# Buffers in two stacks that hand tiles on between the phases of a GLA and conv-FFN block

## The chip, the cores and the metric

The kernel runs on one core of a Trainium2 chip. The time is that of one execution on the device, in microseconds (us), median of several. The engines that matter: PE (TensorE, matmuls and transposes), DVE (VectorE), ACT (ScalarE), POOL (GpSimd), and SP (SyncE), whose queue issues nearly all DMAs in order.

## The reference

One block on a sequence of 2048 tokens with 1024 channels, in float32: a gated linear attention (GLA, 4 heads), then a feed-forward network with a causal convolution of 3 taps, each with a residual, and a last RMS norm.

```python
h = rmsnorm(x, mix_norm_w[i])
y = gla_mixer(h, gla_w_in[j], gla_w_gate2[j], gla_b_gate[j], gla_norm_w[j], gla_w_out[j])
x = x + y.astype(x.dtype)
h = rmsnorm(x, ffn_norm_w[i])
x = x + conv_ffn(h, ffn_w_up[i], ffn_conv_w[i], ffn_conv_b[i], ffn_w_down[i]).astype(x.dtype)
return rmsnorm(x, final_norm_w)

def conv_ffn(h, w_up, conv_w, conv_b, w_down):
    u = causal_dwconv(h @ w_up, conv_w, conv_b)
    g, val = jnp.split(u, 2, axis=-1)
    return (jax.nn.silu(g) * val) @ w_down
```

`w_up` is 1024 x 5632 and `w_down` 2816 x 1024.

## The kernel before

Every float32 matrix product is made of three matmuls: `split` (L206, L207) cuts an operand into a high part (a cast on ACT) and a low part (a subtraction on DVE), and high x low, low x high and high x high are added in PSUM. There are three phases.

**Attention** runs over four blocks of 512 tokens (b = 0 to 3) and, in each, over four heads. The class `Weights` streams all weights of the phase through two rings of buffers of the pool `wp`: "raw" (what DMAs bring, RB = 3) and "w" (the split halves, WB = 18). `hp` has two tiles of 16 KB a partition (the halves of the transposed activations, `hT`), `op` those of the heads' results (`oT`), rows and a ring of 2 KB tiles "s2k" (SB = 15), `sp` and `gc` smaller tiles and constants. `comp_y(b, dh, ...)` multiplies with the output weights in two halves of the channels (`py`, L333 to L335), adds the residual (`x`, L590) and, after the second half, norms the rows for the FFN (`h`, L595). Work that needs such a result much later is put off: `later_do` pushes it on a heap `delayed`, and `adv(us)`, called from attention's matmul helper `mm3` with the estimated time of the matmuls, takes out what is due. One such piece is `blocks`: it transposes the rows on PE (`pt_d`, L604), and for each pair of row tiles makes the seven operands of the next phase (POOL differences `ht`, L621; splits `h_p`, L207) and writes both halves of each to DRAM (`hd`, L617): 14 writes.

**U** multiplies with `w_up` by seven block products p1 to p7 instead of eight. It runs for two halves of the sequence, s = 0 and 1, and in each over 11 groups g; a group has 14 jobs, the products in the order `OPS` = p1, p5, p6, p2, p7, p4, p3 for two column tiles f. A job has 12 matmuls (L714 to L716, in `mm3p`) of one weight operand (`uw_p`) and one activation operand (`h_p`, read from `hd`, L824 and L834). The weights of a group come in four loads (`ur`, L743, ring of 6), POOL makes the sums of blocks (`us`, L748, ring of 5), `split` the halves (ring of 14), five jobs ahead (ULEAD). `ua`, `uc`, `ub` are the products in PSUM. The results are put together in `u`, convolved (`t`, L789 to L793), gated (L798), and the seven operands of the next phase are made by POOL (`as`, L812 to L816) and written to DRAM (`ad`, L802 to L818).

**D** multiplies with `w_down`, again by seven products, in 14 units (product, s) of 11 steps q with 12 matmuls each (`pd`). A step loads its activations (`da`, L905, ring of 7) ten steps ahead and splits them four steps ahead (DLEAD, DLOAD), and for s = 0 the weights too: `ch` is a running combination of blocks in 11 tiles, `dr` a raw block (tag "wr", ring of 6), `dw` their halves (26 buffers).

The Python program gives instructions in this order, and a scheduler then orders each engine's stream by estimated times; the order is fixed when the kernel is built, and each engine, SP's queue too, goes through its own in order. A pool that is opened over the space of a closed one waits for the tiles that lay there. Between the phases, space is handed over pool by pool:

```python
    while delayed:
        heapq.heappop(delayed)[-1]()
    gctx.close()
    ...
    for s in range(NS):
        phase_u(s)
    uctx.close()
```

So `gctx` with all attention pools is closed after the last delayed work, then U's pools `uw`, `uh`, `us` are opened over them; `uctx` is closed after U, then D's `dx`, `dw`, `ds` are opened.

## Time and profile before

| | before |
|---|---|
| time, median of 3 executions (lowest to highest) | 2300.17 us (2300.15 to 2302.63) |
| the profiled execution | 2300.66 us, span 2299.0 us, mean granted PE clock 0.977 |
| first matmul of U, first of D | 985.29 us, 1869.2 us after the start of the span |
| DMA | 322.84 MB, mean 140 GB/s |

Times in the prediction are those of the span of the profiled execution. A row of the timeline has the start, the duration, the engine, the line, the operation, out<-in, how many were put together, and in brackets how long the engine sat idle before it and what released it. In a row of the waits stand the engine and what it waited for, then the sum in us, the number of times and the longest. In the windows, the busy times are those of PE, PEld (weight loads), DVE, ACT and POOL with the number of instructions; then come the clock granted to PE as a share of full speed, the DMA share and GB/s. The rows of DMA issues have KB each and the median us from issue to landing. Line numbers are those of the kernel before; the line numbers of the changed kernel are larger (L714 to L716 become L733 to L735, L604 becomes L607, L595 L598, L207 L210).

### The profile page before, as it was taken

The numbers are of one execution on the slowest core, as the hardware profiler recorded it, in microseconds if no ns is written. First come the engines' busy times: TensorE is split into PE (matmuls) and PEld (weight loads), VectorE is DVE, ScalarE is ACT, GpSimd is POOL, SyncE is SP. The second block draws the span as 40 slices with busy tenths as digits, with TensorE's granted clock in tenths as the row PEclk, the third lists the DMA queues.
The fourth block names the chain that finished last, engine by engine and source line by source line (L and its number), as shares of the span: only waits on it lengthen the run. The fifth ranks groups of instructions, "written<-read, shape, count | busy, mean of one in ns | idle before, by whom it ended". The sixth has DMA issues, their size and how long they took to land. (4 is left out here: it accounts for less than half of the span.)

```text
span 2299.0 us, 31219 instructions
## 1 busy us (share of the span) xinstructions
PE 2167.1 (94%) x10909; PEld 1854.3 (81%) x10909; DVE 1491.9 (65%) x2337; ACT 1164.7 (51%) x2283; POOL 699.8 (30%) x639
## 2 busy tenths in 40 slices
PE   7999899999999999479999999999999959999998
PEld 6898699879987998368888888888888848888887
DVE  5756676667665675447676767676767557557454
ACT  7655765576656665335544545454545434333342
POOL 1000200021101110245555555545454416036000
PEclk9999999999999999789999999999999979999999
DMA  5232663265325532683333337533333268455353
GB/s 161 78 89 84 186 185 96 85 183 175 92 85 173 183 91 66 197 315 110 96 106 101 103 104 282 180 101 106 98 109 94 94 241 277 142 165 188 106 170 119
DMA packets 327885, 322.84 MB, mean 140 GB/s; under 512 B 15686, under 2 KB 262654, under 8 KB 324144
## 3 DMA queue, kind: packets, MB, share of 16 engines
q1 hardware_dynamic: 325280, 312.47, 42.9%
q10 hardware_dynamic: 2448, 8.39, 0.9%
q8 instruction: 85, 1.39, 0.2%
q14 instruction: 72, 0.59, 0.1%
HBM read 234.29 MB, written 86.51 MB: 140 GB/s over the span
## 5 line engine op out<-in xcount | busy, mean ns | idle before, releaser
L714 PE MATMUL ua<-h_p,uw_p 128*128 128x512 f32 x704 | 275.6, 392 | 37.1 <-DMA h_p<-hd_p 36.6
L715 PE MATMUL ua<-h_p,uw_p 128*128 128x512 f32 x704 | 275.5, 391 | 0.0
L716 PE MATMUL ua<-h_p,uw_p 128*128 128x512 f32 x704 | 275.0, 391 | 0.0
L714 PE MATMUL pd_p<-dw_p,da_p 128*128 128x512 f32 x616 | 240.8, 391 | 24.9 <-ACT da_p L206 24.9
L791 DVE SCALAR_TENSOR_TENSOR t<-u,cw,t 128x1024 f32<-128x1024 f32 x176 | 232.0, 1347 | 47.1 <-ACT t L789 30.9
L715 PE MATMUL pd_p<-dw_p,da_p 128*128 128x512 f32 x616 | 240.6, 391 | 0.0
L716 PE MATMUL pd_p<-dw_p,da_p 128*128 128x512 f32 x616 | 240.3, 390 | 0.0
L207 DVE TENSOR_TENSOR uw_p<-us_p,uw_p 128x512 fp32r<-128x512 f32 x176 | 140.1, 806 | 117.8 <-ACT uw_p L206 117.6
L283 POOL TENSOR_TENSOR rstd_o<-var_o,neghalf 128x1 f32<-128x1 f32 x64 | 49.2, 769 | 543.2 <-DVE var_o L281 543.2
L206 ACT CAST uw_p<-us_p 128x512 fp32r<-128x512 f32 x176 | 107.4, 622 | 196.6 <-PE ua L715 43.6
L207 DVE TENSOR_TENSOR da_p<-da_p,da_p 128x512 fp32r<-128x512 f32 x154 | 137.0, 900 | 106.7 <-ACT da_p L206 100.6
L714 PEld LDWEIGHTS ua<-h_p,uw_p 128*128 128x128 f32 x704 | 133.0, 189 | 65.8 <-ACT uw_p L206 32.7
L206 ACT CAST da_p<-da_p 128x512 fp32r<-128x512 f32 x154 | 94.8, 620 | 168.9 <-PE pd_p L715 146.4
L333 PE MATMUL pkv<-wl_q,hTh 128*128 128x384 f32 x512 | 174.6, 341 | 0.4 <-ACT E L421 0.4
L334 PE MATMUL pkv<-wh_q,hTl 128*128 128x384 f32 x512 | 173.5, 339 | 0.0
L335 PE MATMUL pkv<-wh_q,hTh 128*128 128x384 f32 x512 | 172.7, 338 | 0.0
L207 DVE TENSOR_TENSOR uw_p<-ur,uw_p 128x512 fp32r<-128x512 f32 x132 | 116.1, 881 | 67.9 <-ACT uw_p L206 67.9
L206 ACT CAST uw_p<-ur 128x512 fp32r<-128x512 f32 x132 | 81.4, 617 | 148.0 <-PE ua L715 66.1
L714 PEld LDWEIGHTS pd_p<-dw_p,da_p 128*128 128x128 f32 x616 | 116.2, 189 | 49.4 <-ACT da_p L206 25.3
L716 PEld LDWEIGHTS ua<-h_p,uw_p 128*128 128x128 f32 x704 | 133.2, 189 | 27.8
L715 PEld LDWEIGHTS ua<-h_p,uw_p 128*128 128x128 f32 x704 | 133.1, 189 | 27.8
L333 PE MATMUL pr<-wl_r,hTh 128*128 128x256 f32 (+1 forms) x512 | 149.9, 293 | 0.0
(208 smaller groups left out, 5750.2 us busy)
## 6 DMA issues: line engine op xcount, KB each, us to landing
ur<-in_ffn_w_up_dram SPq DMA_DIRECT2D x88, 512.0 KB, 4.2
da_p<-ad_p SPq DMA_DIRECT2D x154, 256.0 KB, 2.7
hd_p<-h_p SPq DMA_DIRECT2D x112, 256.0 KB, 3.6
h_p<-hd_p SPq DMA_DIRECT2D x28, 1024.0 KB, 9.5
ad_p<-as_p SPq DMA_DIRECT2D x88, 256.0 KB, 2.0
dr_p<-in_ffn_w_down_dram SPq DMA_DIRECT2D x77, 256.0 KB, 4.0
ad_p<-t SPq DMA_DIRECT2D x66, 256.0 KB, 2.9
raw_q<-in_gla_w_in_dram SPq DMA_DIRECT2D x128, 128.0 KB, 2.5
```

What stands on the lines that cost most here:

```text
L206: nc.scalar.copy(hi, src)
L207: nc.vector.tensor_sub(lo, src, f32(hi))
L283: nc.gpsimd.tensor_tensor(rstd, var, neghalf, op=ALU.pow)
L333: nc.tensor.matmul(ps_ap, ah, bl, start=(i == 0), stop=False)
L334: nc.tensor.matmul(ps_ap, al, bh, start=False, stop=False)
L335: nc.tensor.matmul(ps_ap, ah, bh, start=False, stop=(i == n - 1))
L714: nc.tensor.matmul(ps_ap, ah, bl, start=(first and i == 0), stop=False, **kw)
L715: nc.tensor.matmul(ps_ap, al, bh, start=False, stop=False, **kw)
L716: nc.tensor.matmul(ps_ap, ah, bh, start=False, stop=(last and i == len(pairs) - 1), **kw)
L791: nc.vector.scalar_tensor_tensor(t, u[:, k:k + TS], cw[:, k, c:c + 1], t, op0=ALU.mult, op1=ALU.add)
```

## The change

Tiles are now kept in two stacks. On the right-hand side lie `wp` (raw ring RB from 3 to 4, "w" ring 18) and `hp`, which stay through all phases; on the left `op` (s2k from 15 to 13).

- `hp`: its two tiles hold U's operands p1 and p5, loaded ahead of the last block's first `comp_y`, and later D's `ch` blocks.
- `sp` and `gc` are closed ahead of the last `comp_y`; over them open `uh` (operands p6 and p2, loaded at once; in D the weights of q < 8) and `uw` (`us` 5 to 4 and copies `cp` 5 to 4).
- U's raw weights and their halves go through `wp`'s rings (raw 6 to 4, halves 14 to 18), so that they can be loaded and split while attention still runs.
- `op` is closed six jobs into U, after the delayed work; over it open `uh2` (operands p7, p4, p3, loaded then) and `us` (`u`, `t`, `as`). `mm3p` calls `adv`, so the last `blocks` run between U's matmuls.
- The sum of p3 is made in the tile of p6.
- In the last group of U, `d_early` loads `ch`, loads and splits D's steps 0 to 3. D's activations lie two steps to a raw tile (8 steps, before 7), their halves in `wp` (9 pairs, before 6); `wr` has 4 buffers (before 6), the weights of q >= 8 have 6 of their own.

The number of matmuls and what is computed stay the same.

```diff
-    WB = 18
-    SB = 15
-    RB = 3
+    WB = 18
+    SB = 13
+    RB = 4
...
+    wp = ctx.enter_context(tc.tile_pool(name="wp", bufs=1, side="right"))
+    hp = ctx.enter_context(tc.tile_pool(name="hp", bufs=1, side="right"))
+    sctx = ExitStack()
+    sp = sctx.enter_context(tc.tile_pool(name="sp", bufs=1, side="right"))
+    gc = sctx.enter_context(tc.tile_pool(name="gc", bufs=1, side="right"))
     gctx = ExitStack()
-    hp = gctx.enter_context(tc.tile_pool(name="hp", bufs=1))
-    sp = gctx.enter_context(tc.tile_pool(name="sp", bufs=1))
-    wp = gctx.enter_context(tc.tile_pool(name="wp", bufs=1))
     op = gctx.enter_context(tc.tile_pool(name="op", bufs=1))
-    gc = gctx.enter_context(tc.tile_pool(name="gc", bufs=1))
...
+    def load_op(s, o, pool, tag, n):
+        t = pool.tile([P, KT, 512], F32R, tag=tag, name=f"h_{s}_{o}", bufs=n)
+        for i in range(2):
+            nc.sync.dma_start(f32(t[:, i * HK:(i + 1) * HK, :]), hd[s, o, i])
+        hop[o] = (t[:, :HK, :], t[:, HK:, :])
...
+        if b + 1 == NB:
+            for o in OPS[:2]:
+                load_op(0, o, hp, "hT", 2)
...
         h2["nw"] = norm_weight(ffn_norm_w, f"ffn{b}")
+        if b + 1 == NB:
+            sctx.close()
+            uh = ctx.enter_context(tc.tile_pool(name="uh", bufs=1, side="right", reuse_waits="tile"))
+            uctx = ExitStack()
+            uw = uctx.enter_context(tc.tile_pool(name="uw", bufs=1, side="right", reuse_waits="tile"))
+            for o in OPS[2:4]:
+                load_op(0, o, uh, o, 1)
         comp_y(b, 1, oT, x1, h2)
-    while delayed:
-        heapq.heappop(delayed)[-1]()
-    gctx.close()
...
             nc.tensor.matmul(ps_ap, ah, bh, start=False, stop=(last and i == len(pairs) - 1), **kw)
+            adv(3 * 0.216 * ps_ap.free_size() / 512)
...
-                    r = uw.tile([P, 2, 512], F32, tag="raw", name=f"ur_{s}_{c}", bufs=6)
+                    r = wp.tile([P, 2, 512], F32, tag="raw", name=f"ur_{s}_{c}", bufs=RB)
...
             elif o == "p3":
-                src = summed(o, f, a12, sums["p6", f], sub)
+                src = sums.pop(("p6", f))
+                sub(src, a12, src)
...
-            hl = [uw.tile([P, 512], F32R, tag="w", name=f"uw{i}_{s}_{f}_{o}", bufs=14) for i in range(2)]
+            hl = [wp.tile([P, 512], F32R, tag="w", name=f"uw{i}_{s}_{f}_{o}", bufs=WB) for i in range(2)]
...
+            if s == 0 and k == 6:
+                while delayed:
+                    heapq.heappop(delayed)[-1]()
+                gctx.close()
+                pools["uh"] = uctx.enter_context(tc.tile_pool(name="uh2", bufs=1, reuse_waits="tile"))
+                pools["us"] = uctx.enter_context(tc.tile_pool(name="us", bufs=1, reuse_waits="tile"))
+                for n in range(4, len(OPS)):
+                    place(OPS[n])
+            if s > 0 and k < 2 * len(OPS) and k % 2 == 0:
+                place(OPS[k // 2])
+            if s == NS - 1 and g == NQ - 1 and f % 2 == 0:
+                d_early(o)
...
+                r = pools["dw"].tile([P, 512], F32, tag="wr", name=f"dr_{o}_{q}_{ij[0]}{ij[1]}", bufs=4)
...
+        if k % 2 == 0:
+            araw["tile"] = wp.tile([P, 2, 512], F32, tag="raw", name=f"da_{o}_{s}_{q}", bufs=RB)
+        r = araw["tile"][:, k % 2, :]
...
+    def d_early(o):
+        if o == "p6":
+            load_chain()
+        elif o == "p2":
+            d_load(4)
+        elif o == "p4":
+            d_prep(2)
+        elif o == "p3":
+            d_prep(4)
```

The order of the instructions on three engines shows what this moves. PE, where the last block of attention ends (`py` with the last output weights, `pt_d_3` the transposes of the last 128 rows, `ua_0` U's first product). Before:

```order
L333 MATMUL py_1_3_11153<-wl_o_1_3_1_11053,oTh_8884 128x512
L334 MATMUL py_1_3_11153<-wh_o_1_3_1_11052,oTl_8885 128x512
L335 MATMUL py_1_3_11153<-wh_o_1_3_1_11052,oTh_8884 128x512
L604 MATMUL pt_d_2_0_11252<-ident,h_3_2_11144 128x128 x4
L604 MATMUL pt_d_2_1_11259<-ident,h_3_2_11144 128x128 x4
L604 MATMUL pt_d_3_0_11266<-ident,h_3_3_11243 128x128 x4
L604 MATMUL pt_d_3_1_11273<-ident,h_3_3_11243 128x128 x4
L714 MATMUL ua_0_11412<-h_0_p_11345,uw_0_0_p_11380 128x512
```

In the changed kernel, the same place up to U's first matmuls, and then the rows around `pt_d_3`, 24 U matmuls further on:

```order
L338 MATMUL py_1_3_11173<-wh_o_1_3_1_11072,oTh_8886 128x512
L733 MATMUL ua_0_11320<-h_p_10781,uw_0_0_p_11288 128x512
L734 MATMUL ua_0_11320<-h_p_10781,uw_0_0_p_11289 128x512
L735 MATMUL ua_0_11320<-h_p_10781,uw_0_0_p_11288 128x512
L607 MATMUL pt_d_2_0_11324<-ident,h_3_2_11164 128x128 x4
L607 MATMUL pt_d_2_1_11331<-ident,h_3_2_11164 128x128 x4
...
L733 MATMUL uc_0_11372<-h_p_10784,uw_0_0_p_11298 128x512
L734 MATMUL uc_0_11372<-h_p_10784,uw_0_0_p_11299 128x512
L735 MATMUL uc_0_11372<-h_p_10784,uw_0_0_p_11298 128x512
L607 MATMUL pt_d_3_0_11376<-ident,h_3_3_11263 128x128 x4
L607 MATMUL pt_d_3_1_11383<-ident,h_3_3_11263 128x128 x4
```

U's p1 jobs and a quarter of its first p5 job have moved ahead of the last transposes. DVE at the same place, from the norm of the third row tile (`h_3_2`) to that of the last (`h_3_3`); `h_3_1_p` are low halves of U's operands. Before:

```order
L595 SCALAR_TENSOR_TENSOR h_3_2_11144<-x_3_2_10937,rstd_d_2_11150,nw_ffn_11016 128x1024
L207 TENSOR_TENSOR h_3_1_p_11172<-hb_0_0_11113,h_3_1_p_11171 128x512
L207 TENSOR_TENSOR h_3_1_p_11182<-ht_1_p_11177,h_3_1_p_11181 128x512
L207 TENSOR_TENSOR h_3_1_p_11188<-ht_1_p_11179,h_3_1_p_11187 128x512
L207 TENSOR_TENSOR h_3_1_p_11196<-hb_0_1_11120,h_3_1_p_11195 128x512
L590 TENSOR_TENSOR x_3_3_10970<-x_3_3_10970,py_1_3_11153 128x512
L207 TENSOR_TENSOR h_3_1_p_11204<-ht_1_p_11201,h_3_1_p_11203 128x512
L207 TENSOR_TENSOR h_3_1_p_11210<-ht_1_p_11193,h_3_1_p_11209 128x512
L281 TENSOR_SCALAR var_d_3_11247<-ssq_d_3_11245 128x1
L595 SCALAR_TENSOR_TENSOR h_3_3_11243<-x_3_3_10970,rstd_d_3_11249,nw_ffn_11016 128x1024
```

In the changed kernel, with `uw` the low halves of U's weights:

```order
L598 SCALAR_TENSOR_TENSOR h_3_2_11164<-x_3_2_10945,rstd_d_2_11170,nw_ffn_11022 128x1024
L210 TENSOR_TENSOR h_3_1_p_11192<-hb_0_0_11133,h_3_1_p_11191 128x512
L210 TENSOR_TENSOR uw_0_0_p_11299<-us_0_p_11296,uw_0_0_p_11298 128x512
L210 TENSOR_TENSOR h_3_1_p_11202<-ht_1_p_11197,h_3_1_p_11201 128x512
L210 TENSOR_TENSOR uw_0_1_p_11305<-us_1_p_11302,uw_0_1_p_11304 128x512
L210 TENSOR_TENSOR h_3_1_p_11208<-ht_1_p_11199,h_3_1_p_11207 128x512
L210 TENSOR_TENSOR uw_0_0_p_11311<-us_0_p_11308,uw_0_0_p_11310 128x512
L210 TENSOR_TENSOR h_3_1_p_11216<-hb_0_1_11140,h_3_1_p_11215 128x512
L593 TENSOR_TENSOR x_3_3_10978<-x_3_3_10978,py_1_3_11173 128x512
L210 TENSOR_TENSOR h_3_1_p_11224<-ht_1_p_11221,h_3_1_p_11223 128x512
L210 TENSOR_TENSOR uw_0_1_p_11317<-us_1_p_11314,uw_0_1_p_11316 128x512
...
L598 SCALAR_TENSOR_TENSOR h_3_3_11263<-x_3_3_10978,rstd_d_3_11269,nw_ffn_11022 128x1024
```

Four splits of `uw` have come between the two norms, and one more stands two rows ahead of them. Last, SP's queue where U ends: before, `da` of step 0 behind the last writes of U's results,

```order
L818 DMA ad_p_10_220<-as_10_p_18406 128x512
L818 DMA ad_p_10_231<-as_10_p_18409 128x512
L818 DMA ad_p_10_275<-as_10_p_18412 128x512
L818 DMA ad_p_10_253<-as_10_p_18415 128x512
L926 DMA xs_18543<-x1d_79 128x1024
L926 DMA xs_18567<-x1d_80 128x1024
L905 DMA da_p_0_0_18437<-ad_p_0_122 128x512
L905 DMA da_p_0_1_18441<-ad_p_1_123 128x512
```

and in the changed kernel, where `ad_p_8` and `ad_p_9` are the results of groups 8 and 9:

```order
L833 DMA ad_p_8_273<-as_8_p_17759 128x512
L833 DMA ad_p_8_251<-as_8_p_17762 128x512
L930 DMA da_p_0_0_18207<-ad_p_0_122 128x512
L930 DMA da_p_0_0_18207<-ad_p_1_123 128x512
L930 DMA da_p_0_2_18210<-ad_p_2_124 128x512
L930 DMA da_p_0_2_18210<-ad_p_3_125 128x512
L917 DMA ch_18156<-in_ffn_w_down_dram 128x512 x2
L817 DMA ad_p_9_208<-t_18_18034 512x1x128
```

The first four steps of D have moved ahead of the writes of the last two groups of U.

More of the change, by code (lines that the diff above doesn't have):

```diff
@@ L149, in hybrid_kernel @@
     cw = cst.tile([P, 4, 2 * NF], F32, name="cw")
-    nwT = gc.tile([P, KT], F32, name="nwT")
+    nwT = cst.tile([P, KT], F32, name="nwT")
     def vectors():
@@ L759, in prep @@
             elif o == "p6":
-                src = summed(o, f, sums["p5", f], a11, sub)
+                src = summed(o, f, sums.pop(("p5", f)), a11, sub)
             elif o == "p7":
@@ L818, in gated, with place @@
                 nc.sync.dma_start(ad[s, o, q], t)
+        def place(o):
+            if o in OPS[:2]:
+                load_op(s, o, hp, "hT", 2)
+            else:
+                load_op(s, o, uh if o in OPS[2:4] else pools["uh"], o, 1)
         load(0)
-        if s == 0:
-            for o in OPS[:2]:
-                for i in range(2):
-                    nc.sync.dma_start(f32(hop[o][i]), hd[s, o, i])
         done = 0
@@ L829, in phase_u @@
                 load(g + 1)
-            if k < 2 * len(OPS) and k % 2 == 0:
-                n = k // 2 + (2 if s == 0 else 0)
-                if n < len(OPS):
-                    for i in range(2):
-                        nc.sync.dma_start(f32(hop[OPS[n]][i]), hd[s, OPS[n], i])
+            if s == 0 and k == 6:
[10 more added lines that the diff above has]
+                d_early(o)
             while done < min(len(jobs), k + ULEAD + 1):
@@ new lines, in hybrid_kernel, with blocks_of, block, load_chain @@
+    dstep = {"loaded": 0, "done": 0}
+    def blocks_of(o):
+        return {"p1": (), "p5": ((1, 2),), "p6": ((2, 2),), "p7": ((2, 2), (1, 2)), "p2": ((2, 1),), "p4": ((2, 1),), "p3": ((2, 2),)}[o]
+    def block(q, i, j):
+        f = 2 * q + i - 1
+        return w_down[f * P:(f + 1) * P, (j - 1) * 512:j * 512]
+    def load_chain():
+        ts = [hp.tile([P, KT, 512], F32R, tag="hT", name=f"ch_{i}", bufs=2) for i in range(2)]
+        for q in range(NQ):
+            chain[q] = f32(ts[q // KT][:, q % KT, :])
+            nc.sync.dma_start(chain[q], block(q, 1, 1))
@@ L904, in load_step @@
-        r = dw.tile([P, 512], F32, tag="ar", name=f"da_{o}_{s}_{q}", bufs=7)
+        if s == 0 and o != "p1":
+            wraw[o, q] = []
+            for ij in blocks_of(o):
+                r = pools["dw"].tile([P, 512], F32, tag="wr", name=f"dr_{o}_{q}_{ij[0]}{ij[1]}", bufs=4)
+                nc.sync.dma_start(r, block(q, *ij))
+                wraw[o, q].append(r)
+        if k % 2 == 0:
+            araw["tile"] = wp.tile([P, 2, 512], F32, tag="raw", name=f"da_{o}_{s}_{q}", bufs=RB)
+        r = araw["tile"][:, k % 2, :]
@@ L905, in load_step, with w_slots @@
         nc.sync.dma_start(r, ad[s, o, q])
         araw[o, s, q] = r
+    def w_slots(o, q):
+        if q < 8:
+            if q % 4 == 0:
+                wgrp[o] = uh.tile([P, KT, 512], F32R, tag=OPS[2 + q // 4], name=f"dw_{o}_{q}", bufs=1)
+            return [wgrp[o][:, q % 4 * 2 + i, :] for i in range(2)]
+        return [pools["dw"].tile([P, 512], F32R, tag="w", name=f"dw{i}_{o}_{q}", bufs=6) for i in range(2)]
     def prep_step(k):
@@ L916, in prep_step, with d_load, d_prep @@
             src = chain[q] if o in ("p1", "p5", "p6", "p4") else r[0]
-            hl = [dw.tile([P, 512], F32R, tag="w", name=f"dw{i}_{o}_{q}", bufs=2 * NQ + 4) for i in range(2)]
+            hl = w_slots(o, q)
             split(hl[0], hl[1], src)
             wops[o, q] = hl
-        hl = [dw.tile([P, 512], F32R, tag="a", name=f"da{i}_{o}_{s}_{q}", bufs=12) for i in range(2)]
+        hl = [wp.tile([P, 512], F32R, tag="w", name=f"da{i}_{o}_{s}_{q}", bufs=WB) for i in range(2)]
         split(hl[0], hl[1], araw.pop((o, s, q)))
         aops[o, s, q] = hl
+    def d_load(n):
+        while dstep["loaded"] < min(len(steps), n):
+            load_step(dstep["loaded"])
+            dstep["loaded"] += 1
+    def d_prep(n):
+        while dstep["done"] < min(len(steps), n):
+            prep_step(dstep["done"])
+            dstep["done"] += 1
+    def d_early(o):
[7 more added lines that the diff above has]
+            d_prep(4)
+    for s in range(NS):
+        phase_u(s)
+    uctx.close()
+    dx = ctx.enter_context(tc.tile_pool(name="dx", bufs=1, reuse_waits="tile"))
+    pools["dw"] = ctx.enter_context(tc.tile_pool(name="dw", bufs=1, side="right", reuse_waits="tile"))
     def load_x1(t):
@@ L989, in hybrid_kernel @@
             k = n * NQ + q
-            while loaded < min(len(steps), k + DLEAD + DLOAD + 1):
-                load_step(loaded)
-                loaded += 1
-            while done < min(len(steps), k + DLEAD + 1):
-                prep_step(done)
-                done += 1
+            d_load(k + DLEAD + DLOAD + 1)
+            d_prep(k + DLEAD + 1)
             if n < NS and q < TT:
```

55 lines of the change are left out of this document (15 added, 40 removed).

## The prediction

> **What bounds the kernel now.** I read the page first, then the waits of PE, then the timeline around the two longest of them.
>
> ```profile
> span 2299.0 us, 31219 instructions
> PE 2167.1 (94%) x10909; PEld 1854.3 (81%) x10909; DVE 1491.9 (65%) x2337; ACT 1164.7 (51%) x2283; POOL 699.8 (30%) x639
> ```
>
> PE, the engine of the matmuls, is busy for 2167.1 of 2299.0 us; 131.9 us are idle. No other engine is above 65%, and the change removes no matmul, so it can win two things only: idle time of PE, and time in which PE runs on a lower clock. PE's waits (sum, times, longest) say where the idle time is:
>
> ```profile
> PE ua L714 <- DMA h_p<-hd_p: 36.6, 2, 32.3
> PE pd_p L714 <- ACT da_p L206: 24.9, 1, 24.9
> PE pq L334 <- DVE wl_q L207: 12.2, 12, 1.8
> PE pt_d L604 <- DVE h L595: 8.9, 4, 7.7
> ```
>
> The first and the fourth lie where attention ends and phase U begins, the second where U ends and D begins. The timeline of PE shows the first place:
>
> ```profile
> 942.30 1.04 PE L604 MATMUL pt_d<-ident,h 128*128 128x128 f32 x8
> 951.01 1.94 PE L604 MATMUL pt_d<-ident,h 128*128 128x128 f32 x8 [7.67 <-DVE h L595]
> 985.29 0.77 PE L714 MATMUL ua<-h_p,uw_p 128*128 128x512 f32 x1 [32.34 <-DMA h_p<-hd_p]
> 985.85 0.63 PE L715 MATMUL ua<-h_p,uw_p 128*128 128x512 f32 x1
> 986.28 0.63 PE L716 MATMUL ua<-h_p,uw_p 128*128 128x512 f32 x1
> ...
> 990.11 0.39 PE L716 MATMUL ua<-h_p,uw_p 128*128 128x512 f32 x1
> 990.34 0.39 PE L714 MATMUL ua<-h_p,uw_p 128*128 128x512 f32 x1
> ...
> 1002.89 0.47 PE L714 MATMUL ua<-h_p,uw_p 128*128 128x512 f32 x1 [4.24 <-DMA h_p<-hd_p]
> ```
>
> Idle there: 7.67 + 32.34 + 4.24 = 44.25 us. From 985.85 matmuls start 0.43 us apart, from 990.11 on 0.23 apart: the 11 that start before 990.11 lose 11 x 0.2 = 2.2 us. The windows (five busy times, granted PE clock, DMA share, GB/s) show the same clock, and that U is full afterwards:
>
> ```profile
> 940.00:950.00 10.00, 3.34 (x19) 2.63 (x17) 9.33 (x10) 5.32 (x10) 6.19 (x5) 0.79 0.64 192
> 980.00:990.00 10.00, 4.71 (x11) 3.82 (x12) 6.16 (x5) 2.37 (x4) 9.84 (x7) 0.50 1.02 397
> 1000.00:1010.00 10.00, 7.11 (x24) 5.78 (x25) 1.00 (x2) 1.11 (x2) 0.00 (x0) 0.83 1.01 423
> 1100.00:1139.00 39.00, 38.74 (x172) 31.75 (x171) 27.00 (x30) 19.14 (x28) 21.74 (x21) 1.00 0.33 101
> 1870.00:1880.00 10.00, 10.00 (x37) 8.10 (x37) 6.61 (x11) 5.17 (x11) 0.00 (x0) 0.79 0.91 301
> ```
>
> A mean of 0.83 over 10 us is 3.4 us at half clock, which loses 1.7 us; the transposes at 951.01 take 1.94 instead of 1.04. So the first place loses 44.25 + 2.2 + 1.7 + 0.9 = 49 us. At the second, 24.9 us are idle, and 0.79 over 1870-1880 is 4.2 us at half clock, which loses 2.1: 27 us in all.
>
> **Start of U.** Why 32.34 us? SP's queue issues in order:
>
> ```profile
> 955.00 13.12 SPq L617 DMA_DIRECT2D hd_p<-h_p  x14
> 968.22 6.63 SPq L743 DMA_DIRECT2D ur<-in_ffn_w_up_dram  x4
> 974.89 3.69 SPq L824 DMA_DIRECT2D h_p<-hd_p  x4
> h_p<-hd_p SPq DMA_DIRECT2D x28, 1024.0 KB, 9.5
> hd_p<-h_p SPq DMA_DIRECT2D x112, 256.0 KB, 3.6
> ```
>
> The last 14 writes of operands go out until 968, the weights follow, and the operand of p1 is asked for at 974.89 and takes some 9.5 us. The change asks for p1, p5, p6 and p2 while attention still multiplies, and these belong to tokens written long before. PE's order then has U's first matmuls directly behind the last py. Ideal: all 49 us go. Three waits are new.
>
> First, the last transposes (of h_3_3) now stand 27 U matmuls later, so PE reaches them at about 943.3 + 27 x 0.227 = 949.5. The h they need is made here:
>
> ```profile
> 944.09 1.70 POOL L621 TENSOR_TENSOR ht_p<-hb,hb 128x512 f32<-128x512 f32 x1
> 941.23 1.77 DVE L207 TENSOR_TENSOR h_p<-hb,h_p 128x512 fp32r<-128x512 f32 x1
> 946.27 0.68 DVE L207 TENSOR_TENSOR h_p<-hb,h_p 128x512 fp32r<-128x512 f32 x1
> 949.58 1.28 DVE L595 SCALAR_TENSOR_TENSOR h<-x,rstd_d,nw_ffn 128x1024 f32<-128x1024 f32 x1 [0.66 <-POOL rstd_d L283]
> ```
>
> Before, h is there at 950.9. After, five splits of U's weights (uw) stand among DVE's splits ahead of it: 5 x 0.68 = 3.4 us if each runs alone, 5 x 1.77 = 8.9 if each runs against POOL, which gets sums of U's weights to make at the same time. So h comes between 954.3 and 959.8, and PE waits 4.8 to 10.3 us; I take 7, in between, since the splits of h_p in these rows show both durations. The bounds are 1.4 us (extra splits all fit into DVE's idle time) and 11.
>
> The Trainium skill ("SBUF — State Buffer", on the shared port pair) says that a DVE operation with two SBUF inputs and a GpSimd operation hold one port pair as an exclusive lock, so that the later one waits in full. The 1.77 beside 0.68 us agrees; by that rule the upper price holds whenever POOL works, the wait is 10 us, and the sum 3 us higher.
>
> A wait of that length halves the clock again, if it goes as at 985.29: 2.3 us.
>
> Second, U's tiles for convolution and p7, p4, p3 need the space of attention's pool, so they wait for the last 14 writes: these are issued over 13.12 us, now behind four weight loads that wait for a free raw buffer. PE gets past p1, p5, p6, p2 (96 matmuls, 21.8 us) at about 943.3 + 21.8 + 7 + 2.3 = 974.4, goes on with the p5 and p1 of the next group (48 matmuls, 10.9 us), and needs p7 at about 985.3. The writes of h_3_3 follow h by 4 us, as before (950.9 to 955.0), and 2 more for the weights ahead of them: with h at 957, 963; 13 us of issue, 3.6 to land and 9.5 to load p7 make 989 to 990. So 5 us of idle, in one or two pieces, and 3 for single waits (p1 of the next group needs a bank whose result has no tile yet): 8, from 0 to 16. Sum left: 7 + 2.3 + 8 = 17, from 1.4 to 29. **Gain 32 us, from 20 to 47.**
>
> **U to D.** Before, the loads of D's first activations stand in SP's queue behind the last writes of U, and these wait for POOL:
>
> ```profile
> 1843.30 4.88 DVE L791 SCALAR_TENSOR_TENSOR t<-u,cw,t 128x1024 f32<-128x1024 f32 x4 [1.22 <-ACT t L789]
> 1854.17 1.22 DVE L798 TENSOR_TENSOR t<-t,t 128x1024 f32<-128x1024 f32 x1 [1.12 <-ACT t L793]
> 1857.14 5.33 SPq L818 DMA_DIRECT2D ad_p<-as_p  x4
> 1860.42 1.71 POOL L816 TENSOR_TENSOR as_p<-t 128x512 f32<-128x512 f32 x1
> 1863.49 7.95 SPq L905 DMA_DIRECT2D da_p<-ad_p  x9
> 1868.55 0.62 ACT L206 CAST da_p<-da_p 128x512 fp32r<-128x512 f32 x1 [10.79 <-DMA da_p<-ad_p]
> ```
>
> After, activations of steps 0 to 3 are loaded ahead of the writes of group 9, and their splits end inside U's last jobs. Four steps keep PE busy for 4 x 12 x 0.227 = 10.9 us. In that time DVE has U's last convolutions (12 us before, from 1843.3 to 1855.4) and the splits of steps 4 and on (2 x 0.68 us each). That may leave PE waiting for 2 to 3 us; I take 2: **gain 25 us**, from 15 (step 4 waits for the whole tail, and the clock falls again) to 27.
>
> **Attention.** A fourth raw buffer (RB) loads weights one tile earlier. It can win part of the 12.2 us of pq. The clock falls there too, at the transition between blocks 1 and 2 for instance:
>
> ```profile
> 502.00:512.00 10.00, 8.49 (x20) 4.74 (x21) 5.64 (x9) 6.15 (x12) 0.55 (x1) 0.50 0.97 265
> ```
>
> I take a third of the 12.2, **4 us**, from -2 (two s2k buffers fewer hold up splits) to 9 (half of the waits, 6, and 3 of the clock), since weights that come one tile earlier still go through the same splits.
>
> **Smaller buffers in D.** The weights of p7 need two raw tiles a step. Landing 4.0, POOL 1.3 and the split 1.3 make a round of some 6.6 us, with issue 7.5:
>
> ```profile
> L915 POOL TENSOR_TENSOR dr_p<-dr_p,dr_p x11: 1283/1298/1745, 1946.6 to 2043.0; 128x512 f32<-128x512 f32 x11
> dr_p<-in_ffn_w_down_dram SPq DMA_DIRECT2D x77, 256.0 KB, 4.0
> ```
>
> Six buffers give a step each 2.5 us, four one each 3.75, where PE takes 2.72. Over 11 steps D falls 11.3 us behind, of which its lead of four steps covers 10.9. **Cost 2 us**, from 0 to 11.
>
> **Sum.** The profiled execution took 2300.66 us, 0.5 above the median of 2300.17. 2300.7 - 32 - 25 - 4 + 2 = 2241.7, say **2242**.
>
> **Rivals.** *The new waits take most of the start of U* (0.22): DVE and POOL are the bound there, at 29 us left instead of 17, and U to D keeps 8: some 2260. For it speaks that DVE is busy for 9.33 of 10 us at 940 in the windows; against it, that POOL stands idle for 3.8 of those 10.
>
> *Everything goes, and the clock in attention too* (0.18): 8 us left at U's start, 9 more in attention: 2224. The Trainium skill ("TensorE: Matmul & The Clock Gate", Part 1) says that a window of activity of about 3.4 us decides over the half clock. The 3.4 us at half clock after a gap of 4.24 agree; by that rule a first wait shorter than the window keeps the clock, and the sum is 2.3 us lower.
>
> *Slower* (0.06): in steady U the raw weights have four buffers instead of six, so every load waits for the same group's splits, and SP's queue stands.
>
> ```profile
> 1154.45 0.37 SPq L743 DMA_DIRECT2D ur<-in_ffn_w_up_dram  x1
> 1160.81 0.68 DVE L207 TENSOR_TENSOR uw_p<-ur,uw_p 128x512 fp32r<-128x512 f32 x1
> 1153.57 0.39 PE L714 MATMUL uc<-h_p,uw_p 128*128 128x512 f32 x1
> ```
>
> The second raw tile comes free with the split of p4 (1161.5), lands some 5 us later, and PE needs its sum for p5 in the next group, 39 us after 1153.6, split (1.3) and summed (1.3) before: 23 us of slack. If POOL or SP used these up, each further us would come in 21 groups: 4 us make 84, and 2242 + 84 = 2326. It decides from 23 + 59/21 = 26 us of delay, 59 us being the gain of the sum. The slack speaks against it.
>
> *Not what it says* (0.04): the loads wait for space after all and one of the two stalls stays: 2242 + 32 or + 25, about 2270 and more.
>
> **Numbers.** My forecast (0.50) has a range of its own from 2232 to 2254. With the first two rivals and the bounds (47, 27 and 9 won: 2218; 20, 15 and 0 won and 11 lost: 2277) the range is 2218 to 2277. This kernel's time can be told from no change beyond some 0.2%, 4.6 us. Faster: 0.50 + 0.22 + 0.18 + 0.03 = 0.93; within: 0.01; slower: 0.06.
>
> **What would show it.** The wait of ua on h_p at 32 us and of pd_p on da_p at 25 us are gone from PE's waits; a wait of pt_d on h of about 7 us stands some 6 us after U's first matmul, and one on p7's load or on u some 35 us later; half clock is granted for under 10 us at U's start and not at D's. I am wrong if single waits in U on uw_p or ur come once a group, if dr_p holds up PE in p7, or if the transitions in attention grow.

## The result, and the profile after

The changed kernel took 2248.38 us (median of 4 executions, 2246.88 to 2249.95) against 2300.18 us before (2300.15 to 2302.63): a ratio of 0.9772, with a 95% interval from 0.9755 to 0.9789. The forecast was 2242 with a range from 2218 to 2277. The profiled execution took 2248.04 us, its mean granted PE clock was 0.990 (0.977 before).

The first part of the page of the changed kernel:

```profile
span 2246.3 us, 31132 instructions
PE 2172.5 (97%) x10909; PEld 1852.2 (82%) x10909; DVE 1519.6 (68%) x2337; ACT 1161.0 (52%) x2283; POOL 702.9 (31%) x639
```

PE is idle for 2246.3 - 2172.5 = 73.8 us instead of 131.9. But its busy time went up, from 2167.1 to 2172.5, with the same 10909 matmuls and a higher mean clock. That second number is the first sign of something that the forecast did not contain. PE's waits (sum, times, longest) in the changed kernel:

```profile
PE pt_d L607 <- DVE h L598: 10.6, 4, 7.5
PE pq L337 <- DVE wl_q L210: 10.3, 12, 1.9
PE uc L733 <- DVE u L886: 7.7, 2, 5.7
```

The 32.3 us on `h_p` and the 24.9 us on `da_p` are gone. New among the long ones are 7.5 us on `h` and 5.7 us on `u`. PE's timeline shows both, and the places where the phases meet:

```profile
937.46 0.39 PE L338 MATMUL py<-wh_o,oTh 128*128 128x512 f32 x1
937.69 0.40 PE L733 MATMUL ua<-h_p,uw_p 128*128 128x512 f32 x1
...
952.45 1.94 PE L607 MATMUL pt_d<-ident,h 128*128 128x128 f32 x8 [7.54 <-DVE h L598]
...
1034.36 0.80 PE L733 MATMUL uc<-h_p,uw_p 128*128 128x512 f32 x1 [5.68 <-DVE u L886]
...
1816.22 0.39 PE L733 MATMUL pd_p<-dw_p,da_p 128*128 128x512 f32 x1
...
1819.60 0.39 PE L735 MATMUL uc<-h_p,uw_p 128*128 128x512 f32 x1
1819.83 0.39 PE L733 MATMUL pd_p<-dw_p,da_p 128*128 128x512 f32 x1
```

U's first matmul starts 0.23 us after attention's last. D's first three matmuls start from 1816.22 on, ahead of U's last twelve, and its next one 0.23 us after U's last. Both seams are closed, and what idles now ends 15 and 97 us behind the first one. The windows (PE, PEld, DVE, ACT, POOL; granted clock; DMA share, GB/s) for these two waits, and for a stretch of D:

```profile
940.00:950.00 10.00, 4.90 (x22) 3.71 (x20) 9.41 (x9) 4.21 (x9) 8.71 (x6) 0.91 0.73 216
950.00:960.00 10.00, 7.55 (x25) 6.38 (x26) 8.13 (x9) 7.15 (x14) 5.78 (x5) 0.58 0.93 266
...
1010.00:1020.00 10.00, 10.00 (x45) 8.16 (x44) 10.00 (x10) 6.21 (x12) 6.02 (x5) 1.00 0.32 93
1020.00:1030.00 10.00, 8.67 (x38) 6.64 (x36) 10.00 (x8) 4.14 (x7) 9.84 (x7) 1.00 0.43 146
1030.00:1040.00 10.00, 5.64 (x13) 4.51 (x14) 9.05 (x9) 3.46 (x4) 5.60 (x6) 0.67 0.36 106
...
1998.00:2028.00 30.00, 30.00 (x134) 24.86 (x133) 16.61 (x24) 9.46 (x17) 11.51 (x9) 1.00 0.65 219
```

At both waits DVE is full while PE stands: 9.41 and 8.13 of 10 us at the first, 10.00, 10.00 and 9.05 at the second. The clock of 0.91 and 0.58 makes (0.09 + 0.42) x 2 x 10 = 10.2 us at half clock, 0.67 makes 6.6 us, part of it while PE still stands. The last row is p7 of D, full.

Cut at the same matmuls, the two traces compare as follows (us; starts of matmuls from the two timelines; the 617th matmul of U lies where steady U has begun in both):

| stretch | before | after | difference | forecast |
|---|---|---|---|---|
| start to attention's last `py` | 942.07 | 937.46 | -4.6 | -4 |
| to U's 617th matmul | 192.8 | 166.2 | -26.6 | -32 |
| to U's last matmul | 709.1 | 716.0 | +6.9 | 0 |
| to D's 133rd matmul | 57.8 | 29.5 | -28.3 | -25 |
| rest of D | 388.7 | 388.7 | 0 | +2 |
| end | 8.6 | 8.5 | -0.1 | 0 |
| span | 2299.0 | 2246.3 | -52.7 | -59 |

So four questions were open: do the early tiles do it at both seams, what makes the wait of 7.5 and the one of 5.7, what wins 4.6 us in attention, and where do 6.9 us in steady U come from.

### The profile page after: what moved, and what is told of

The parts are those of the page before. It is cut to its first block, busy times and chain, and to the rows that moved or that the text cites. A ratio compares the mean times of both kernels' runs of the same rounds, so it can differ in the third digit from the quotient of the medians.

```text
span 2246.3 us, 31132 instructions
## 1 busy us (share of the span) xinstructions
PE 2172.5 (97%) x10909; PEld 1852.2 (82%) x10909; DVE 1519.6 (68%) x2337; ACT 1161.0 (52%) x2283; POOL 702.9 (31%) x639
## 4 chain that ended last, share of the span: by engine, by line
PE 80%; DVE 7%; ACT 6%; issue 3%; DMA 3%; POOL 2%; SPq 0%; DVEq 0%; POOLq 0%; ACTq 0%
PE ua L733 7%; PE ua L734 7%; PE ua L735 7%; PE pd_p L735 6%; PE pd_p L734 6%; PE pd_p L733 6%; PE uc L733 4%; PE uc L734 3%; PE uc L735 3%; PE pkv L336 2%; PE pkv L338 2%; PE pkv L337 2%; PE pr L337 2%; PE pr L338 2%; PE pr L336 2%
## 5 line engine op out<-in xcount | busy, mean ns | idle before, releaser
L806 DVE SCALAR_TENSOR_TENSOR t<-u,cw,t 128x1024 f32<-128x1024 f32 x176 | 244.2, 1418 | 40.4 <-ACT t L804 23.3
L210 DVE TENSOR_TENSOR uw_p<-us_p,uw_p 128x512 fp32r<-128x512 f32 x176 | 158.1, 900 | 118.4 <-ACT uw_p L209 118.4
L210 DVE TENSOR_TENSOR da_p<-da_p,da_p 128x512 fp32r<-128x512 f32 x154 | 127.7, 844 | 136.9 <-ACT da_p L209 134.8
L733 PE MATMUL uc<-h_p,uw_p 128*128 128x512 f32 x352 | 142.4, 404 | 8.9 <-DVE u L886 7.7
L337 PE MATMUL pr<-wh_r,hTl 128*128 128x256 f32 (+1 forms) x512 | 146.3, 286 | 0.4 <-DVE hTl L210 0.3
L210 DVE TENSOR_TENSOR uw_p<-ur,uw_p 128x512 fp32r<-128x512 f32 x132 | 129.3, 992 | 24.7 <-ACT uw_p L209 24.7
```

What stands on the lines that cost most here:

```text
L210: nc.vector.tensor_sub(lo, src, f32(hi))
L337: nc.tensor.matmul(ps_ap, al, bh, start=False, stop=False)
L733: nc.tensor.matmul(ps_ap, ah, bl, start=(first and i == 0), stop=False, **kw)
L806: nc.vector.scalar_tensor_tensor(t, u[:, k:k + TS], cw[:, k, c:c + 1], t, op0=ALU.mult, op1=ALU.add)
```

## The experiments

All ratios are to the kernel before, measured on the same chip as the experiment. Each edit is made to the changed kernel. A time of one run is called so.

### The two seams: are the tiles the cause?

**p1 loaded late.** p1 and p7 of the first half exchange their tiles, so that U's first operand lies over attention's `op` pool; that pool is closed ahead of U's first job.

```diff
-            for o in OPS[:2]:
+            for o in ("p7", "p5"):
...
-            if s == 0 and k == 6:
+            if s == 0 and k == 0:
...
-                for n in range(4, len(OPS)):
+                load_op(s, "p1", pools["uh"], "p7", 1)
+                for n in range(5, len(OPS)):
```

> p1 and p7 of the first half exchange their tiles: p7 is loaded early into the tile of hp, p1 waits for the space of attention's pool, which is closed ahead of U's first job. p5, p6, p2, the weights and their splits stay early. Theory A (the tile that is free early is what starts U early): U begins with p5 (24 matmuls), then PE waits for p1 until about 985 to 990, where it was loaded in time before; 20 to 30 us more, 2268 to 2278. Theory B (the early splits of weights are what counts): within 8 us of 2248.

Measured: 2269.81 us (one run), 21 us more than the change. PE's timeline:

```profile
954.62 1.73 PE L607 MATMUL pt_d<-ident,h 128*128 128x128 f32 x7 [13.64 <-DVE h L598]
...
956.21 0.77 PE L733 MATMUL uc<-h_p,uw_p 128*128 128x512 f32 x1
...
987.01 0.80 PE L733 MATMUL ua<-h_p,uw_p 128*128 128x512 f32 x1 [22.98 <-DMA h_p<-hd_p]
```

and SP's queue:

```profile
967.32 10.42 SPq L620 DMA_DIRECT2D hd_p<-h_p  x12
977.79 3.51 SPq L646 DMA_DIRECT2D h_p<-hd_p  x5
```

The operand is asked for behind the last writes again, as before the change, and the first matmul of p1 starts at 987 us, where it started at 985. U itself begins at 956.21 with p5, whose 24 matmuls are done when PE stands for p1. The raw weights and splits are still early, and they don't close the seam: it takes the early tile of the operand. Whether the early weights are needed beside it was not tested.

**D's first activations loaded late.** Steps 0 and 1 of D read their activations from a tile that lies over U's `t`, the early calls are gone (`ch` is asked for behind U's last group), and `wr` shrinks to 2 buffers to make room.

```diff
-            if s == NS - 1 and g == NQ - 1 and f % 2 == 0:
-                d_early(o)
...
-                r = pools["dw"].tile([P, 512], F32, tag="wr", name=f"dr_{o}_{q}_{ij[0]}{ij[1]}", bufs=4)
+                r = pools["dw"].tile([P, 512], F32, tag="wr", name=f"dr_{o}_{q}_{ij[0]}{ij[1]}", bufs=2)
...
-        if k % 2 == 0:
+        if k == 0:
+            araw["tile"] = pools["dx"].tile([P, 2, 512], F32, tag="first", name="da_first")
+        elif k % 2 == 0:
...
+    load_chain()
     uctx.close()
```

> D's activations of steps 0 and 1 get a tile in a pool that opens when U is closed, on the place of U's tiles t, instead of a raw tile that lives through both phases; the early calls are taken out (they alone leave the order of all engines as it is) and wr has 2 buffers instead of 4. Theory A (what removes the stall is that the tile is free early, and with it the place of the load in the queue): PE waits for da at D's start 20 to 27 us with the clock falling to half after it, 2270 to 2277. Theory B (weights and the other steps loaded early cover it): under 5 us more. Beyond the start of D, two buffers of wr can cost up to 15 us in the units p5 to p3, which the starts of D's units show apart.

Measured: 2295.54 us, ratio 0.9978 (0.9968 to 0.9987). PE's timeline and, behind it, SP's queue:

```profile
1847.37 0.79 PE L733 MATMUL pd_p<-dw_p,da_p 128*128 128x512 f32 x1 [28.30 <-ACT da_p L209]
```

```profile
1836.64 3.77 SPq L833 DMA_DIRECT2D ad_p<-as_p  x4
...
1842.95 0.86 SPq L930 DMA_DIRECT2D da_first<-ad_p  x2
```

The stall is back (28.3 us) as soon as the tile must wait for U's end. Taking out the `d_early` calls alone was not run: built so, the order of all five engines stays as it is, since the scheduler moves loads with free tiles ahead by itself. Two raw buffers for `wr` are too few: the unit of p7 takes 45.1 us instead of 29.9, PE waits for `dw` (9.4 us in six waits). With four PE loses nothing there, as the row of D above shows.

### The wait for h

**No sums of U's weights in the first group.** POOL's sums for group 0 of the first half are left out; a raw block stands in for each. DVE has the same instructions in the same order.

```diff
-            if o == "p5":
+            if s == 0 and g == 0:
+                src = {"p1": a11, "p2": a12, "p4": a22, "p5": a21, "p6": a11, "p7": a21, "p3": a12}[o]
+            elif o == "p5":
```

> Leaves out POOL's sums of weight blocks in group 0 of the first half (us): a raw block is split in place of each sum. The order on DVE stays: five splits of weights still stand ahead of the last x. Theory A (contention with POOL sets the length of the first wait): the wait of pt_d for h falls from 7.5 us to 3 to 5. Theory B (the number of splits sets it): it stays 6.5 to 7.5 us.

Measured: 2246.68 us (one run). The wait for `h` is 4.00 us instead of 7.54. DVE in the changed kernel, from the third split of U's weights to `h`:

```profile
941.32 1.77 DVE L210 TENSOR_TENSOR h_p<-ht_p,h_p 128x512 fp32r<-128x512 f32 x1
943.02 1.77 DVE L210 TENSOR_TENSOR uw_p<-us_p,uw_p 128x512 fp32r<-128x512 f32 x1
944.71 1.75 DVE L210 TENSOR_TENSOR h_p<-hb,h_p 128x512 fp32r<-128x512 f32 x1
946.38 0.68 DVE L593 TENSOR_TENSOR x<-x,py 128x512 f32<-128x512 f32 x1
...
948.07 0.68 DVE L210 TENSOR_TENSOR uw_p<-us_p,uw_p 128x512 fp32r<-128x512 f32 x1
...
951.02 1.28 DVE L598 SCALAR_TENSOR_TENSOR h<-x,rstd_d,nw_ffn 128x1024 f32<-128x1024 f32 x1 [1.61 <-POOL rstd_d L286]
```

and with the sums left out:

```profile
943.23 0.68 DVE L210 TENSOR_TENSOR uw_p<-ur,uw_p 128x512 fp32r<-128x512 f32 x1
943.83 0.68 DVE L210 TENSOR_TENSOR h_p<-ht_p,h_p 128x512 fp32r<-128x512 f32 x1
944.43 0.68 DVE L210 TENSOR_TENSOR uw_p<-ur,uw_p 128x512 fp32r<-128x512 f32 x1
...
948.84 1.28 DVE L598 SCALAR_TENSOR_TENSOR h<-x,rstd_d,nw_ffn 128x1024 f32<-128x1024 f32 x1 [0.66 <-POOL rstd_d L286]
```

The same split takes 1.77 us beside a POOL sum and 0.68 us without. The one at 948.07 in the changed kernel is short too, since POOL stands just then:

```profile
948.89 1.58 POOL L779 TENSOR_TENSOR us_p<-ur,us_p 128x512 f32<-128x512 f32 x1 [1.29 <-ACT h_p L209]
```

The 3.54 us that go are nearly half of the first wait. Most of them are this contention; 0.95 us are POOL's own order, since `rstd`, which `h` needs, stood behind that sum (1.61 us of waiting, 0.66 without). What remains, 4.00 us, fits the number of instructions (five splits at 0.68 make 3.4), which no run takes away by itself. The shorter wait also came with less half clock: 0.99 and 0.84 are granted from 940 to 950 and from 950 to 960 us, which is 3.4 us instead of 10.2. The whole run gains little, though: PE now comes earlier to p7, waits 1.1 us for its load, and the wait of 5.7 us stays.

**The last transposes put off by 7 us.** If PE only met `h` later, the wait would go.

```diff
-                later_do(NLY, lambda tt=tt, rows=rows: blocks(b, tt, rows, h2))
+                later_do(NLY + (7.0 if b + 1 == NB and tt + 1 == NT else 0.0), lambda tt=tt, rows=rows: blocks(b, tt, rows, h2))
```

> The last transposes (h_3_3) are put off by another 7 us of estimated matmul time: they stand 60 instead of 27 matmuls behind U's start, so PE reaches them at about 952.3, when h_3_3 is there. The wait of 7.5 us and the 3 us at half clock after it go. Theory A (next comes the chain of writes and the load of p7, which landed at about 985, 2.5 us ahead of PE, and the DVE that is full from 1010 to 1035): PE waits later for h_p or u instead, 0 to 4 us gained, 2244 to 2248. Theory B (the wait is the bound there by itself): 10 us gained, 2238.

Measured: 2253.41 us, ratio 0.9787 (0.9772 to 0.9802): no gain, which neither theory foresaw. At U's start PE no longer waits for `h`, but PE's timeline has another in its place:

```profile
976.31 0.79 PE L733 MATMUL uc<-h_p,uw_p 128*128 128x512 f32 x1 [14.31 <-ACT uw_p L209]
```

POOL and ACT show why:

```profile
961.81 1.26 POOL L762 TENSOR_TENSOR us_p<-ur 128x512 f32<-128x512 f32 x1 [10.55 <-DMA ur<-in_ffn_w_up_dram]
```

```profile
973.56 0.62 ACT L209 CAST h_p<-ht_p 128x512 fp32r<-128x512 f32 x1 [6.28 <-POOL ht_p L624]
974.08 0.61 ACT L209 CAST uw_p<-ur 128x512 fp32r<-128x512 f32 x1
```

In this order a sum of raw weights (`us`) stands on POOL ahead of the operands' differences (`ht`). It waits 10.55 us for a weight load, the differences come late, and ACT's casts of weights queue behind a cast that needs them. Putting work off moved it behind another queue's wait.

### The wait for u

**No operand sums for two groups.** POOL's sums `as` of groups 0 and 1 of the first half are left out.

```diff
+            for o in ("p5", "p6", "p3", "p7") if s == 0 and q < 2 else ():
+                nc.sync.dma_start(tiles1(ad[s, o, q]), a11)
-            for o, fn, x, y in (("p5", "add", a21, a22), ("p6", "sub", None, a11), ("p3", "rsub", None, a12), ("p7", "sub", a11, a21)):
+            for o, fn, x, y in () if s == 0 and q < 2 else (("p5", "add", a21, a22), ("p6", "sub", None, a11), ("p3", "rsub", None, a12), ("p7", "sub", a11, a21)):
```

> Leaves out the four sums that POOL makes of the activations of groups 0 and 1 of the first half (as), and writes another block in their place. Theory A (DVE falls behind at U's start because its splits wait for POOL's operations: 1.3 to 1.8 us each instead of 0.68 between 1013 and 1031): the wait of 5.7 us at 1028.7 for u shrinks to under 2 us, the half clock after it goes, 5 to 9 us less. Theory B (it is the order alone: splits of later groups stand ahead of the sum that PE waits for): the wait stays 4 us or more.

Measured: 2246.69 us (one run), and the wait is 3.10 us instead of 5.68, between what the theories named:

```profile
1033.90 0.50 PE L733 MATMUL uc<-h_p,uw_p 128*128 128x512 f32 x1 [3.10 <-DVE u L888]
```

DVE in the changed kernel ahead of the `u` that PE waits for:

```profile
1018.22 3.48 DVE L210 TENSOR_TENSOR uw_p<-ur,uw_p 128x512 fp32r<-128x512 f32 x2
...
1022.22 5.18 DVE L210 TENSOR_TENSOR uw_p<-us_p,uw_p 128x512 fp32r<-128x512 f32 x4
1027.33 2.31 DVE L806 SCALAR_TENSOR_TENSOR t<-u,cw,t 128x1024 f32<-128x1024 f32 x1
1029.56 1.75 DVE L210 TENSOR_TENSOR uw_p<-ur,uw_p 128x512 fp32r<-128x512 f32 x1
1031.23 2.28 DVE L806 SCALAR_TENSOR_TENSOR t<-u,cw,t 128x1024 f32<-128x1024 f32 x1
1033.61 0.69 DVE L886 TENSOR_TENSOR u<-uc,c 128x512 f32<-128x512 f32 x1
```

Five splits and two convolution steps stand ahead of one sum of 0.69 us. Without POOL's `as`, DVE's order is the same and some of it is shorter:

```profile
1020.34 2.38 DVE L210 TENSOR_TENSOR uw_p<-ur,uw_p 128x512 fp32r<-128x512 f32 x2
...
1031.78 1.27 DVE L806 SCALAR_TENSOR_TENSOR t<-u,cw,t 128x1024 f32<-128x1024 f32 x1
```

The two splits take 1.1 us less, the second convolution step 1.0 and the four splits 0.5 (4.69 instead of 5.18): 2.6 us, which is what the wait lost. So a little under half of this wait is contention with `as`. Some splits stay long (1.76 us for the one ahead of that step); what POOL's sums of weights add and what is the order alone, this run doesn't divide.

### Attention's 4.6 us

**Prefetch as deep as before, ring of 4 kept.**

```diff
-                while self.loaded < self.emitted // 2 + RB:
+                while self.loaded < self.emitted // 2 + 3:
```

> The ring has four raw tiles as in the changed kernel, but attention loads its weights only three tiles ahead, as before. Theory A (the tile that is loaded earlier is what wins time in attention): the last py starts at about 942 as before instead of 937.5, 4 to 5 us more in all. Theory B (the other tiles of the new layout, or their place, win it): the last py stays at 937 to 939, time within 2 us of 2248.

Measured: 2247.32 us, ratio 0.9761 (0.9745 to 0.9777), the last `py` at 937.32 us. So the deeper prefetch wins nothing that these profiles show. The end of attention varies by itself: in five other kernels with the order of the changed one (swap, pad, mirror, aligned and 128 bytes up, below) the last `py` starts between 937.05 and 939.47 us. In the waits of attention, `pq` on `wl_q` went from 12.2 to 10.3 us with the change, `pq` on `wh_q` (L333 before) from 4.6 to 0.3, and `pk` on `vlz` rose from 0.5 to 3.8; without the deeper prefetch they stand at 10.1, 0.5 and 3.8. But only 1.5 of the 4.6 us are waits; by 3.1 PE's busy time fell (893.9 in the first 942.3 us before, 890.8 in the first 937.7 after). Half clock was granted for 27.3 us there before and 23.9 after, which is about half of that. What the gain comes from (the fourth buffer itself, the order that came out, or where the clock fell) stays open.

### Steady U's 6.9 us

Over the stretch of 709.1 and 716.0 us, PE is idle for 5.3 us before and 3.3 after; busy is 703.8 and 712.7. So the idle time shrank by 2.0, and the matmuls themselves take 8.9 us more. The timeline of the changed kernel at the seam from p2 (`ub`) to p7 (`ua`) shows it:

```profile
1529.69 0.39 PE L735 MATMUL ub<-h_p,uw_p 128*128 128x512 f32 x1
...
1530.14 0.39 PE L734 MATMUL ub<-h_p,uw_p 128*128 128x512 f32 x1
...
1530.59 0.40 PE L733 MATMUL ua<-h_p,uw_p 128*128 128x512 f32 x1
...
1531.98 0.40 PE L733 MATMUL ua<-h_p,uw_p 128*128 128x512 f32 x1
```

Six matmuls from 1530.59 to 1531.98 are 0.232 us apart, the last ones of p2 0.225. Over all of U, p5, p6 and p2 are 0.227 apart, p1 0.228, and p7, p4 and p3 0.233. These three are 72 of a group's 168 matmuls, so some 1320 of the 3079 in this stretch: at 6.2 ns each they make 8.2 of the 8.9 us. They alone lie on the left-hand side. The first theory was the region in memory, the second the exact address.

**Another region.** The pool of p7, p4 and p3 is opened behind `us` and a pad of 40 bytes, 37 KB higher up.

```diff
-                pools["uh"] = uctx.enter_context(tc.tile_pool(name="uh2", bufs=1, reuse_waits="tile"))
                 pools["us"] = uctx.enter_context(tc.tile_pool(name="us", bufs=1, reuse_waits="tile"))
+                pools["us"].tile([P, 10], F32, tag="pad", name="pad")
+                pools["uh"] = uctx.enter_context(tc.tile_pool(name="uh2", bufs=1, reuse_waits="tile"))
```

> The three operand tiles of p7, p4 and p3 lie 37 KB higher in each partition (at 40,704 instead of 3,680 bytes), the tiles u, t, as below them. In the changed kernel every matmul that streams p7, p4 or p3 starts 0.233 us after the one before, every other 0.227; 72 of a group's 168 matmuls are such, so 72 x 0.0063 = 0.45 us a group and 10 us over 22 groups. Theory A (the place of the streamed operand in SBUF decides): the spacing of some or all three goes to 0.227, and the time falls by 3 to 10 us to about 2238 to 2245. Theory B (these jobs are slow because of what the other engines do beside them): spacing stays 0.233, time 2248 within 2 us.

Measured: 2248.94 us, ratio 0.9769 (0.9754 to 0.9784); p7, p4 and p3 stay at 0.233. The region is not it.

**A pad of 32 bytes** below the left stack.

```diff
+    cst.tile([P, 8], F32, name="pad")
```

> 32 bytes of padding ahead of the left-hand stack: p7, p4 and p3 start at a multiple of 64 bytes (3,712) instead of 32 beyond one. Theory A1 (alignment): spacing 0.227, about 10 us less. Theory A2 (the region of the address) and theory B (the work beside it): spacing stays 0.233, time 2248 within 2 us.

Measured: 2251.73 us (one run); 0.234: a shift of 32 bytes cures nothing.

**p1 and p4 exchange tiles** in the second half.

```diff
-            if o in OPS[:2]:
+            if s == 1 and o == "p1":
+                load_op(s, o, pools["uh"], "p4", 1)
+            elif o in OPS[:2] or (s == 1 and o == "p4"):
```

> In the second half of the sequence p1 and p4 exchange their operand tiles: p4 lies where p1 was, in the tile of hp that lives through all phases, p1 in the pool over attention's old space. Theory A (the place of the streamed operand): in that half p4 starts a matmul every 0.227 us and p1 every 0.233. Theory B (the work beside these jobs): p4 stays at 0.233 and p1 at 0.227 to 0.229. p1's load now waits for a tile that is used until late in the first half, which may cost up to 10 us once.

Measured: 2251.53 us (one run). In the second half p4 is now at 0.2273 and p1 at 0.2328. So where the operand lies decides, not the product.

**The stacks change sides**; `hp`, `sp`, `gc`, `op` and the later pools likewise.

```diff
-    wp = ctx.enter_context(tc.tile_pool(name="wp", bufs=1, side="right"))
+    wp = ctx.enter_context(tc.tile_pool(name="wp", bufs=1))
...
-                pools["uh"] = uctx.enter_context(tc.tile_pool(name="uh2", bufs=1, reuse_waits="tile"))
+                pools["uh"] = uctx.enter_context(tc.tile_pool(name="uh2", bufs=1, side="right", reuse_waits="tile"))
```

> The two stacks change sides and nothing else: raw tiles and weight halves lie at 4 to 57 KB, p1, p5, p6, p2 from 57 to 122 KB, and attention's pool and after it p7, p4, p3 at the top, 180 to 229 KB; the order of all engines is that of the changed kernel. In the kernel before, weights at 27 to 56 KB and operands at 66 to 181 KB gave 0.227 us from matmul to matmul for all seven products. Theory A (the low addresses are what makes a streamed operand slow): p7, p4 and p3 go to 0.227 and the time to about 2238. Theory B (a streamed operand is slow when it lies in the other half of SBUF from the weights): p7, p4 and p3 stay at 0.233, time 2246 to 2250. Attention's products move too, so up to 5 us either way come from there.

Measured: 2247.26 us, ratio 0.9764 (0.9751 to 0.9778); on the other side of memory the three are at 0.233 as before. It is not the operand's own address either: in the changed kernel operands that lie at 480 modulo 512 bytes are at 0.227 and those at 96 at 0.233, in this one it is the reverse, and the weights lie at 480 there and at 96 here. With the tiles' addresses of all these kernels beside the spacings, one rule was left: what counts is how the address of the streamed operand lies to that of the weights. The next run was made to test it.

**Aligned.** A small tile (`ssq`, four buffers) moves from the constants to D's pool, so that the left stack begins 128 bytes lower; the order on all engines is the same.

```diff
-        ssq = cst.tile([P, 2], F32, tag="ssq2", name=f"ssqf_{t}", bufs=4)
+        ssq = dx.tile([P, 2], F32, tag="ssq2", name=f"ssqf_{t}", bufs=4)
```

> Four small tiles move out of the first pool, so that the left-hand stack begins 128 bytes lower (3,552 instead of 3,680); the order of all engines stays. Over six kernels so far, the matmuls with 512 columns start 0.227 us apart wherever the address of the streamed operand and that of the next weights differ by a multiple of 512 bytes, and 0.232 to 0.234 apart wherever they don't. Here p7, p4, p3 against their weights, and py's weights against oT, come to a multiple of 512. Theory A (that difference decides): all seven products of U and py at 0.227, 10 us less in U and 3 to 4 us less in attention: 2234 to 2239. Theory B (the pool or the region, the agreement is chance): 0.233 stays, 2246 to 2250.

Measured: 2242.44 us (median of 5, 2240.44 to 2246.48), ratio 0.9738 (0.9725 to 0.9752), whose interval has no overlap with that of the change. The same place of its timeline:

```profile
1531.47 0.39 PE L733 MATMUL ua<-h_p,uw_p 128*128 128x512 f32 x1
...
1532.83 0.39 PE L733 MATMUL ua<-h_p,uw_p 128*128 128x512 f32 x1
```

Six matmuls take 1.36 us: 0.227 each. From its 617th matmul to its last, U takes 711.6 us here and 711.5 in the next run, and 715.6 to 719.0 in the changed kernel and all other runs. In this stretch the spacings below 0.245 us have a mean of 0.2269 (0.2297 in the changed kernel, 0.2268 before), which over 3080 matmuls gives 8.7 us back. PE's busy time is 706.3 us instead of 712.7.

Less came out than the 13 to 14 us expected. In U, pauses came back: what the longer spacings cost rose from 8.2 to 12.5 us, of which the profile counts 3.3 and 5.3 as idle. And in attention no gain is seen: the last `py` starts at 939.12 us. (The profiled execution, 2246.48 us, is the slowest of the five.) The row of waits on `u` over the whole run reads

```profile
PE uc L733 <- DVE u L886: 10.4, 11, 6.3
```

against 7.7, 2, 5.7 in the change. It seems that a PE that runs faster meets `u` from DVE too early; that was not tested.

**128 bytes up instead of down.**

```diff
+    cst.tile([P, 32], F32, name="pad")
```

> The left-hand stack begins 128 bytes higher (3,808): streamed operand and weights of p7, p4, p3 differ by a multiple of 256 bytes, not of 512. Theory A1 (a multiple of 256 is enough): 0.227, some 2235. Theory A2 (it takes a multiple of 512): 0.232 to 0.234, 2246 to 2252.

Measured: 2242.84 us (one run), p7 and p4 at 0.2267, p3 at 0.228 as before the change. Here the difference of the addresses is a multiple of 256 bytes but not of 512, so 256 is enough.

## Why the prediction held, and where it did not

- **Both seams close because tiles are free early.** Right: a late tile for p1 brings 23 us of wait back at U's start, one for D's activations 28.3 us at D's start.
- **First new wait, 7 us.** Right in size and place: 7.54. Of its two parts, leaving out the sums shows contention with POOL (4.00 us left); that the rest is the number of splits was not tested by itself. The half clock around it (10.2 us, of which PE stood for a part) lost about 3 us where 2.3 were put. By the rule of the Trainium skill that the prediction weighed ("SBUF — State Buffer", on the shared port pair) with every split at the upper price, the wait would have been 10 us. The splits at 1.77 agree with the rule, and those at 0.68 don't speak against it: POOL was not working all the time.
- **Second new wait, 8 us.** The size was near by luck, the mechanism was wrong. It was put on p7's load, around 985 us. There PE waits 2.2 us in small pieces, none of them for p7, whose load lands in time. What came is 5.68 us from 1028.7 on, for `u`, because DVE had been full since 1010 (2.6 us of the wait are contention with POOL's `as`), and 6.6 us at half clock, of which some 5.9 fall on matmuls and lose about 3. The prediction counted which transfers would be late, not how much DVE work piles up when seven products follow at full speed.
- **Start of U as a whole.** 26.6 us won instead of 32, within the 20 to 47 given. Left are 7.5 + 3 + 2.2 + 5.7 + 3 = 21.4 us of the 49, where 17 were put; the clock behind the second wait is what the sum had no term for. Another 1.4 us is an estimate from the spacing: 233 of these 617 matmuls belong to p7, p4 and p3. The sign named for it, half clock for under 10 us at U's start, failed: it was granted for some 17 us. And the condition of the second rival, a wait so short (under 3.4 us) that the clock stays, is not borne out: without the `as` sums, a wait of 3.10 us was followed by 3.4 us at half clock.
- **U to D.** 28.3 instead of 25: the 2 us left over for DVE did not come, and the other 1.3 is more than the bound of 27 named.
- **Attention.** 4.6 instead of 4, by luck: the reason given, weights asked for a tile earlier, fell, and most of the gain is not in waits. What does it is open.
- **Smaller buffers in D.** 0 instead of 2. The round of 6.6 to 7.5 us was too long: with two buffers each step needs one round, and the 45.1 us of that unit over its 11 steps make 4.1 us each (an estimate). Four buffers then allow a step every 2.05 us, less than PE's 2.72; with two, 15 us are lost.
- **Steady U.** Nothing was put there and 6.9 us came: 8.9 from where the stacks begin, less 2.0 of waits. This is the largest miss: the prediction took it for granted that a matmul takes the same time wherever its operand lies. It is larger than the 6.4 us by which the forecast fell short, because the other errors (5.4 us too much gain at U's start; 3.3, 0.6 and 2 too little at D's start, in attention and in D) nearly cancel. Of the rivals, the slower one (four raw buffers starve every group) did not occur: PE waits for no load of weights in steady U.
